# The end of a transformer block rebuilt: last products row block by row block, right halves prepared early, eight output buffers

## The chip, the cores and the metric

The kernel runs on one core of one Trainium2 chip. It is one launch that computes one whole layer. The metric is device time in microseconds (us), the median of several executions of the same program.

A core has five engines that run their own instruction queues and wait for each other through semaphores: TensorE (PE in the profile) multiplies matrices into PSUM banks, VectorE (DVE) and ScalarE (ACT) do elementwise work, GpSimd (POOL) does slower elementwise work, and SyncE (SP) issues DMA transfers between the core's SBUF and the device's memory. Each engine runs its queue strictly in order: an instruction that waits holds up everything behind it on that engine.

## What is computed

One layer on an input x of 1024 positions by 1024 channels: a normalised, modulated input goes through a state-space mixer and a chunked attention, then a convolutional feed-forward network, and a last RMS norm. Only the end matters here:

```python
def rmsnorm(x, w):
    y = x * lax.rsqrt(jnp.mean(x * x, axis=-1, keepdims=True) + EPS)
    return y * w
...
        x = x + g_f * conv_ffn(h, w_up[l], ffn_conv_w[l], w_down[l])
    return rmsnorm(x, final_norm_w)
```

The last step of `conv_ffn` is a product of a (1024 x 2816) matrix with `w_down` (2816 x 1024). Its result is multiplied by the gate `g_f`, x is added, and every row of 1024 numbers is divided by its root mean square and weighted with `final_norm_w`. A row's scale is known only when both of its halves of 512 columns are complete.

## The kernel before

**The product.** The down projection is done as a Strassen-like scheme: the (1024 x 2816) by (2816 x 1024) product is cut into 2 x 2 blocks, and seven products of half size, in the order P1, Q5, Q6, Q7, Q4, P3, P2, stand in place of eight. Each product works on 11 steps of 128 along the contracted dimension (`KH`), loaded in six pieces m = 0 to 5 of two steps, the last of one (`NM`, `kn`). Each result is four row blocks of 128 x 512 numbers in four PSUM banks (`banks("d")` and `banks("e")` alternate). For precision every float32 operand is split into a high part (ACT, line 85) and a low part (DVE, line 86), and `mm3` (lines 76 to 78) issues three matmuls per step and row block: high by high, high by low, low by high. `split_pair` makes the split parts of one piece in tiles of a ring of five (`ring`), so a split can start only when TensorE has done with the piece that used the ring tile before.

**The rows.** There are eight row blocks of 128 positions and two column halves. Four lists of four tiles of 128 x 512 gather the results: `q5` is the right half of row blocks 4 to 7 and is complete after Q7; `u3` is the right half of row blocks 0 to 3 and is complete after Q4; `u2` is the left half of row blocks 4 to 7 and is complete after P3; `p1` is the left half of row blocks 0 to 3 and is complete after P2. `gate` (lines 1408 to 1413) multiplies a tile by the gate `gf` and adds x, which a DMA brings into one of two buffers `xts`.

**The last product.** `product("P2", W, tail=True)` issues steps 0 to 7 and returns the last three (pieces 4 and 5) in `last`. At the end a loop over the four row blocks of rows 0 to 3 issues for each row block its nine matmuls, a multiplication by the gate into `e` (line 1493), the addition to `p1` (line 1494) and `final`.

**`final`** (lines 1415 to 1424) squares both halves on ACT into the output tile with a running sum (line 1419; each is an ACTIVATE and a small ACTIVATION_READ_ACCUMULATOR), combines the two sums on DVE (line 930) and raises to the power -0.5 on POOL (line 931, in `rstd2`), scales and weights each half in one DVE instruction with the scale and the weights `fnr` (line 1422), and sends each half out with a DMA on SP (line 1424). Its output tile is one of three, `fins`.

**What sets the order.** The program states dependencies; a planner that simulates a timeline orders each engine's queue, so instructions of the end may be placed ahead of or between others than the text has them, and the nine matmuls of the four row blocks may be mixed. Two things pin the order by hand: `tc.issue_after`, and the wrapper `InOrder`, which while its `on` is true makes each instruction of an engine follow the one before it in the text (its issues are then recorded under line 58).

Of the kernel before, what the change touches and what calls it, by code (L numbers as in the profile page):

```python
# [12 lines left out]
AF = mybir.ActivationFunctionType  # L13
ALU = mybir.AluOpType
PSUM = bass.MemoryType.PSUM

P = 128
# [47 lines left out]
def tile_block(ctx: ExitStack, tc: tile.TileContext, x, crep, pk, w_ada, w_first, w_ft, w_z,  # L65
               w_out, w_up, w_down, bias, fnw, out, dbg=None):
    nc = tc.nc
    V, A, T = (InOrder(tc, e) for e in (nc.vector, nc.scalar, nc.tensor))
    G = nc.gpsimd
# [36 lines left out]
    def stat(n=1):  # L106
        if stc[0] + n > 64:
            stc[0] = 0
        a = st1[:, stc[0]:stc[0] + n]
        stc[0] += n  # L110
        return a
# [15 lines left out]
    def raw_tile(n=1024):  # L127
        rawc[0] += 1
        return raws[:, rawc[0] % 2, 0:n]
# [199 lines left out]
    for hh in range(2):  # L329
# [4 lines left out]
        for kt in range(KT):  # L334
            if hh == 0:
# [4 lines left out]
                t = raw_tile(768)  # L340
# [50 lines left out]
    ya = yp.tile([P, NT, 512], F32, tag="y", name="ya")  # L391
# [147 lines left out]
    xs = xsp.tile([P, NT, 512], F32, name="xs")  # L539
# [60 lines left out]
    halves = [slice(0, 512), slice(512, 1024)]  # L600
# [202 lines left out]
    def ssd_y(c, xdt, xdd, cb, ms_):  # L803
        cs = slice(c * P, (c + 1) * P)
        prev, cur = state[c % 2], state[(c + 1) % 2]
        ydp = ssd_tile("ydp")
        for h in range(8):
            pe(T.matmul, ydp[:, h * 64:h * 64 + 64], ms_[h // 4][:, h % 4, :],
               xdt[:, h * 64:h * 64 + 64], start=True, stop=True)
        y = sp.tile([P, 512], F32, tag="yy", bufs=2, name="yy")  # L810
        G.tensor_tensor(h8(y), h8(xs[:, c, :]),
                        pkt[:, DSK:DSK + 8].unsqueeze(2).to_broadcast([P, 8, 64]), ALU.mult)
        t = sp.tile([P, 512], F32, tag="yt", bufs=2, name="yt")
        if c > 0:
            yop = ssd_tile("yop")
            for g in range(2):
                pe(T.matmul, yop[:, g * 256:g * 256 + 256], ct_[g][:, cs], prev[:, g * 256:g * 256 + 256],
                   start=True, stop=True)
        if c < NT - 1:
            stp = ssd_tile("stp")  # L820
            for g in range(2):
                pe(T.matmul, stp[:, g * 256:g * 256 + 256], cb[:, 2 + g, :],
                   xdd[:, g * 256:g * 256 + 256], start=True, stop=True)
            if c > 0:
                G.tensor_tensor(h8(cur), h8(prev), hb("cd", c), ALU.mult)
                V.tensor_tensor(cur, stp, cur, ALU.add)
            else:
                A.activation(cur, stp, AF.Copy)
        V.tensor_tensor(y, ydp, y, ALU.add)
        if c > 0:  # L830
            V.tensor_tensor(h8(t), h8(yop), hb("ea", c), ALU.mult)
            V.tensor_tensor(y, y, t, ALU.add)
        return y, t
# [21 lines left out]
    def kn(m):  # L855
        return min(2, KH - 2 * m)

    gd = {}
    for m in range(NM):
        for n, names in (("x", ("b11",)), ("y", ("t1", "t3")), ("z", ("t2", "t4", "b21", "b22"))):  # L860
            t = gd[n, m] = dram.tile([kn(m), P, len(names), 512], F32, name=f"g{n}{m}")
# [66 lines left out]
    def rstd2(m):  # L928
        ms, r = stat(), stat()
        V.scalar_tensor_tensor(ms, m[0], EPS, m[1], op0=ALU.add, op1=ALU.add)  # L930
        G.tensor_tensor(r, ms, mhalf[:, 0:1], ALU.pow)  # L931
        return r
# [4 lines left out]
    for c in range(NT):  # L937
        y, t = ssd_y(c, *pre)
# [85 lines left out]
    def wsplit(src, n=2):  # L1024
# [5 lines left out]

    PRODS = dict(P1=(0, "b11", "X"), P2=(1, "b21", "X"), Q4=(2, "t4", "Y"), Q5=(4, "t1", "Z"),
                 Q6=(5, "t2", "Y"), Q7=(6, "t3", "Y"), P3=(7, "b22", "Z"))

    class Unit:
# [23 lines left out]
        def product(self, p, post=True):  # L1058
            _, n, t = PRODS[p]
            start = t not in self.ps  # L1060
            if start:
                self.ps[t] = (psz if t == "Z" else ps3).tile([P, 512], F32, tag=t, bufs=2, name="u" + t)
            ps, w, h = self.ps[t], self.w[p], hb_[n]
            for kt in range(4):
                c = slice(kt * P, (kt + 1) * P)
                mm3(ps, w[:, 0, c], w[:, 1, c], h[0][:, kt, :], h[1][:, kt, :],
                    start and kt == 0, kt == 3, not start)
            if post:
                self.post(p)

        def post(self, p):
# [12 lines left out]
            elif p == "Q7":  # L1084
                V.tensor_tensor(self.v[:, 512:S], ps, self.v[:, 0:512], ALU.subtract)
                V.tensor_tensor(self.v[:, 512:S], self.v[:, 512:S], self.ps["Z"], ALU.subtract)
            elif p == "Q4":
# [78 lines left out]
    row = lambda u, o: (lambda: u.sums((o,)))  # L1166
# [51 lines left out]
    lo = [u.prep("Q7", "Q4", True) for u in units]  # L1218
# [31 lines left out]
    def buf(name, n=D):  # L1250
        if name not in bufs:
            home = next(h for h in HOME if name in HOME[h][1])
            pool, names = HOME[home]
            t = pool.tile([P, 1024 * (1 if home == "s0" else 4 if pool is htp else 2)], F32,
                          tag="a" if pool is hp else home, bufs=2 if pool is hp else 1,
                          name="dn" + home)
            o = 0
            for g in names:
                w = 512 if g.endswith("_5") else 1024
                bufs[g] = t[:, o:o + w]  # L1260
                o += w
        return bufs[name][:, 0:n]
# [80 lines left out]

    gf, fnr = (t[:, 0:2, :].rearrange("p a b -> p (a b)") for t in (ya, xs))
    q5 = [ya[:, 2 + st, :] for st in R4]
    fins = [t[:, j:j + 2, :].rearrange("p a b -> p (a b)") for t, j in ((xs, 2), (xs, 4), (ya, 6))]
    xts = [xs[:, 6 + j, :] for j in range(2)]
    BANK = dict(zip(("e2", "e3", "d0", "d1", "d2", "d3", "e0", "e1"), range(8)))
    for t in BANK:
# [2 lines left out]
    def banks(t):  # L1352
        return [ps4.tile([P, 512], F32, tag=f"{t}{st}", name="dn") for st in R4]
# [31 lines left out]
    def step(ps, ab, k, sts):  # L1385
        a, b = (t[:, :, k % 2, :] for t in ab)
        for st in sts:
            c = slice(st * P, (st + 1) * P)
            mm3(ps[st], b[:, 0, c], b[:, 1, c], a[:, 0, :], a[:, 1, :], k == 0, k == KH - 1)
# [14 lines left out]
    def xt_():  # L1404
        xc[0] += 1
        return xts[xc[0] % 2]

    def gate(t, st, dh):
        V.tensor_tensor(t, t, gf[:, halves[dh]], ALU.mult)
        x = xt_()  # L1410
        with tc.issue_after(last_load[0]):
            nc.sync.dma_start(x, x1d[st * P:(st + 1) * P, halves[dh]])
        V.tensor_tensor(t, t, x, ALU.add)

    def final(st, lo, hi):
        t = fins[st % 3]
        m = [stat(), stat()]
        for dh, src in enumerate((lo, hi)):
            A.activation(t[:, halves[dh]], src, AF.Square, scale=1.0 / 32.0, accum_out=m[dh])
        r = rstd2(m)  # L1420
        for dh, src in enumerate((lo, hi)):
            V.scalar_tensor_tensor(t[:, halves[dh]], src, r, fnr[:, halves[dh]], op0=ALU.mult,
                                   op1=ALU.mult)
            nc.sync.dma_start(out[st * P:(st + 1) * P, halves[dh]], t[:, halves[dh]])

    def rows(ts):
        return [t[:, 512 * j:512 * j + 512] for t in ts for j in range(2)]
# [37 lines left out]
    u3 = rows([buf("u30"), buf("u31")])  # L1465
    for st in R4:
        V.tensor_tensor(u3[st], X[st], u2[st], sub)
    for st in R4:
        V.tensor_tensor(u2[st], u2[st], q5[st], ALU.add)
        V.tensor_tensor(q5[st], u3[st], q5[st], sub)  # L1470
    for st in R4:
        gate(q5[st], 4 + st, 1)
    nc.sync.dma_start(fnr, fnw)
    X = banks("d")
    product("Q4", X)
    for st in R4:
        V.tensor_tensor(u3[st], u3[st], X[st], ALU.add)
    for st in R4:
        gate(u3[st], st, 1)
    Z = banks("e")  # L1480
    product("P3", Z)
    W = banks("d")
    last = product("P2", W, tail=True)
    for st in R4:
        V.tensor_tensor(u2[st], u2[st], Z[st], ALU.add)
    for st in R4:
        gate(u2[st], 4 + st, 0)
        final(4 + st, u2[st], q5[st])
    for st in R4:
        for ab, k in last:  # L1490
            step(W, ab, k, (st,))
        e = xt_()
        V.tensor_tensor(e, W[st], gf[:, halves[0]], ALU.mult)
        V.tensor_tensor(p1[st], p1[st], e, ALU.add)
        final(st, p1[st], u3[st])
    es_s.close()
    es_ht.close()
    es_l.close()
# [51 lines left out]
```

## Time and profile before

| what | before |
|---|---|
| median of 3 runs | 1222.43 us (1222.42 to 1225.11) |
| profiled execution, span from first to last instruction | 1221.2 us |
| mean granted TensorE clock | 0.993 |
| POOL busy in the span | 174.3 us |
| multiplications of two 128 x 512 tiles on POOL (lines 708, 811) | 1.12 and 1.36 us mean |
| `fnr` load (line 1473): issued, landed | 1045.4 us, 7.7 us later |
| right-half squares of row blocks 4, 5, 6 (line 1419) | 1130.65, 1135.86, 1136.49 us |

The profiled execution's own time is known by its span alone, 1221.2 us; the median of the runs is 1.2 us above that, for what lies around the first and the last instruction.

A row of the timeline gives start, duration, engine, line, operation, output tile <- input tiles, shapes, and in brackets the idle time before it with what ended that. Rows of one kind that follow each other are merged (x2, x4), and their duration then reaches from the first start to the last end. Output tiles called `dn` on PE are PSUM banks; `cg` holds `p1`, `cv` holds `u2`, `st` the row sums and scales; `xs` and `ya` are two large tiles that hold `gf`, `fnr`, `q5`, `fins` and the buffers `xts`; `dnH` holds `u3` among other things. A window row gives, for one stretch, the busy time of each engine with its count of instructions, then granted clock, share of the DMA engines and GB/s.

### The profile page before, as it was taken

The numbers are of one execution on the slowest core, as the hardware profiler recorded it, in microseconds if no ns is written. First come the engines' busy times: TensorE is split into PE (matmuls) and PEld (weight loads), VectorE is DVE, ScalarE is ACT, GpSimd is POOL, SyncE is SP. The second block draws the span as 40 slices with busy tenths as digits, with TensorE's granted clock in tenths as the row PEclk, the third lists the DMA queues.
The fourth block names the chain that finished last, engine by engine and source line by source line (L and its number), as shares of the span: only waits on it lengthen the run. The fifth ranks groups of instructions, "written<-read, shape, count | busy, mean of one in ns | idle before, by whom it ended". The sixth has DMA issues, their size and how long they took to land.

```text
span 1221.2 us, 15631 instructions
## 1 busy us (share of the span) xinstructions
PE 1167.3 (96%) x5802; PEld 974.5 (80%) x5802; DVE 928.8 (76%) x1402; ACT 592.0 (48%) x993; POOL 174.3 (14%) x166
## 2 busy tenths in 40 slices
PE   5998899989999989999999999999999999999995
PEld 3877787878889978888788888888888888888884
DVE  7846454686697678657999988898889769666976
ACT  4636454664243766676544543344343445433443
POOL 1205463672000125200000000000000000000001
PEclk9999999999999999999999999999999999999998
DMA  9722211311476200141223223322233278633533
GB/s 331 259 56 63 66 54 46 111 58 51 164 246 229 88 18 35 61 147 52 70 104 118 93 107 113 129 79 86 95 129 112 108 250 305 242 126 116 171 114 137
DMA packets 56395, 150.86 MB, mean 124 GB/s; under 512 B 5632, under 2 KB 5760, under 8 KB 54912
## 3 DMA queue, kind: packets, MB, share of 16 engines
q1 hardware_dynamic: 49264, 125.49, 30.4%
q10 hardware_dynamic: 7056, 24.38, 5.0%
q8 instruction: 45, 0.74, 0.2%
q14 instruction: 30, 0.25, 0.1%
HBM read 116.56 MB, written 29.10 MB: 119 GB/s over the span
## 4 chain that ended last, share of the span: by engine, by line
PE 82%; DVE 9%; ACT 3%; issue 2%; DMA 2%; POOL 1%; SPq 0%; DVEq 0%; POOLq 0%; ACTq 0%
PE dn L76 6%; PE dn L77 6%; PE dn L78 6%; PE wops L699 5%; PE uY L76 4%; PE uY L78 4%; PE uY L77 4%; PE uX L78 3%; PE uX L76 3%; PE uZ L77 3%; PE uZ L76 3%; PE uX L77 3%; PE uZ L78 3%; PE s L76 3%; PE s L77 3%; PE s L78 3%
## 5 line engine op out<-in xcount | busy, mean ns | idle before, releaser
L77 PE MATMUL dn<-w 128*128 128x512 f32 x308 | 112.6, 391 | 0.0
L76 PE MATMUL dn<-w 128*128 128x512 f32 x308 | 112.6, 391 | 0.0
L931 POOL TENSOR_TENSOR st<-st,mhalf 128x1 f32<-128x1 f32 x16 | 10.9, 683 | 696.1 <-DVE st L930 684.6
L419 POOL TENSOR_SCALAR p<-p,st 128x640 f32<-128x640 f32 (+4 forms) x64 | 99.0, 1560 | 43.7 <-DVE st L418 36.4
L78 PE MATMUL dn<-w 128*128 128x512 f32 x308 | 103.7, 390 | 0.0
L76 PE MATMUL uY<-tH,w 128*128 128x512 f32 x248 | 97.2, 392 | 0.0
L77 PE MATMUL uY<-tL,w 128*128 128x512 f32 x248 | 97.0, 391 | 0.0
L78 PE MATMUL uY<-tH,w 128*128 128x512 f32 x248 | 96.9, 391 | 0.0
L85 ACT ACTIVATE w<-ya 128x1024 fp32r<-128x1024 f32 (+1 forms) x41 | 39.2, 956 | 87.4 <-PE uY L78 84.2
L699 PE MATMUL wops<-hH,yhl 128*128 128x512 f32 x224 | 74.1, 399 | 2.9 <-DVE yhl L86 1.5
L76 PEld LDWEIGHTS dn<-w 128*128 128x128 f32 x308 | 57.8, 188 | 12.9
L78 PEld LDWEIGHTS dn<-w 128*128 128x128 f32 x308 | 57.8, 188 | 12.8
L77 PEld LDWEIGHTS dn<-w 128*128 128x128 f32 x308 | 57.8, 188 | 12.7
L85 ACT ACTIVATE w<-xs 128x1024 fp32r<-128x1024 f32 (+1 forms) x41 | 39.1, 953 | 37.3 <-PE uY L78 33.3
L78 PEld LDWEIGHTS uY<-tH,w 128*128 128x128 f32 x248 | 46.5, 188 | 10.5
L76 PEld LDWEIGHTS uY<-tH,w 128*128 128x128 f32 x248 | 46.6, 188 | 10.3
L77 PEld LDWEIGHTS uY<-tL,w 128*128 128x128 f32 x248 | 46.6, 188 | 10.2
L413 DVE CUSTOM_DVE_ANT_0 p<-s,bias 128x640 f32<-128x640 f32 (+4 forms) x64 | 40.4, 651 | 17.5 <-PE tp L445 5.2
L76 PE MATMUL s<-hH,wh 128*128 128x512 f32 x128 | 50.1, 392 | 2.2 <-ACT xst L518 2.0
L86 DVE TENSOR_TENSOR pt<-tp,pt 128x512 fp32r<-128x512 f32 (+2 forms) x72 | 41.5, 595 | 13.1 <-ACT pt L85 12.8
L699 PEld LDWEIGHTS wops<-hH,yhl 128*128 128x128 f32 x224 | 41.8, 188 | 12.2 <-DVE yhl L86 1.9
L1101 DVE SCALAR_TENSOR_TENSOR a<-cv,pkt,a 128x1023 f32<-128x1023 f32 (+1 forms) x40 | 51.0, 1278 | 0.1
(453 smaller groups left out, 3388.9 us busy)
## 6 DMA issues: line engine op xcount, KB each, us to landing
wos<-in_w_ada_dram SPq DMA_DIRECT2D x25, 512.0 KB, 4.5
gz<-a ACTq DMA_DIRECT2D x10, 1024.0 KB, 5.0
ya<-in_w_up_dram SPq DMA_DIRECT2D x11, 768.0 KB, 4.1
xs<-in_w_up_dram SPq DMA_DIRECT2D x11, 768.0 KB, 4.2
adat<-in_w_ada_dram SPq DMA_DIRECT2D x16, 512.0 KB, 5.9
raws<-in_w_ft_dram SPq DMA_DIRECT2D x14, 512.0 KB, 4.0
gy<-a ACTq DMA_DIRECT2D x10, 512.0 KB, 2.6
qk<-in_x_dram SPq DMA_DIRECT2D x8, 512.0 KB, 6.6
```

The lines of the kernel that those rows point to most:

```text
L76: T.matmul(ps, lh, rh, start=start, stop=False, skip_group_check=more)
L77: T.matmul(ps, lh, rl, start=False, stop=False, skip_group_check=more)
L78: T.matmul(ps, ll, rh, start=False, stop=stop, skip_group_check=more)
L85: i = A.activation(hi, src, AF.Copy) if ehi is A else ehi.tensor_copy(hi, src)
L86: return i, elo.tensor_tensor(lo, src, f32(hi), ALU.subtract)
L413: V.tensor_tensor_reduce(out=dst, in0=src, in1=bsl, scale=-1.0, scalar=3e38, op0=ALU.add, op1=ALU.min, accum_out=nm)
L419: G.tensor_scalar(pv_, pv_, rr, None, op0=ALU.mult)
L699: i = op(*a, **k)
L931: G.tensor_tensor(r, ms, mhalf[:, 0:1], ALU.pow)
L1101: V.scalar_tensor_tensor(a[:, j:S], c[:, 0:S - j], w[2 - j], a[:, j:S], op0=ALU.mult, op1=ALU.add)
```

## The change

Four edits, all in the code after the feed-forward's first half.

- The 36 last matmuls of P2 are issued in the order of the text: row block 0 with all nine, then 1, 2, 3 (`T.on`).
- The right halves of all row blocks are squared as soon as they are gated, and multiplied in place by the right half of `fnr` on POOL (`right_half`). The statement of the `fnr` load stands ahead of that.
- `final` squares only the left half. Its right half is scaled by ACT (an activation Copy with a scale per row), its left half still by DVE. The right half is sent first.
- The output tile of each row block is its own, in memory that earlier products no longer need (`buf("a11_0")` and so on), in place of three in turn; squares go into six `junk` tiles, and `e` is one of those in place of a buffer of `xts`.

In the built program the `fnr` load has the same place in SP's queue as before, DVE's order differs only from the first line 1422 on, ACT's gets the early squares and the copies, POOL's gets eight multiplications ahead of its last eight powers, and PE's differs in the last 36 matmuls alone.

```diff
-    fins = [t[:, j:j + 2, :].rearrange("p a b -> p (a b)") for t, j in ((xs, 2), (xs, 4), (ya, 6))]
+    junk = [t[:, j, :] for t, j in ((xs, 2), (xs, 3), (xs, 4), (xs, 5), (ya, 6), (ya, 7))]
...
-    def final(st, lo, hi):
-        t = fins[st % 3]
-        m = [stat(), stat()]
-        for dh, src in enumerate((lo, hi)):
-            A.activation(t[:, halves[dh]], src, AF.Square, scale=1.0 / 32.0, accum_out=m[dh])
-        r = rstd2(m)
-        for dh, src in enumerate((lo, hi)):
-            V.scalar_tensor_tensor(t[:, halves[dh]], src, r, fnr[:, halves[dh]], op0=ALU.mult,
-                                   op1=ALU.mult)
-            nc.sync.dma_start(out[st * P:(st + 1) * P, halves[dh]], t[:, halves[dh]])
+    jc, sq = [0], {}
+
+    def junk_():
+        jc[0] += 1
+        return junk[jc[0] % 6]
+
+    def square(row, dh, src):
+        sq[row, dh] = stat()
+        A.activation(junk_(), src, AF.Square, scale=1.0 / 32.0, accum_out=sq[row, dh])
+
+    def right_half(row, src):
+        square(row, 1, src)
+        G.tensor_tensor(src, src, fnr[:, halves[1]], ALU.mult)
+
+    def final(row, lo, hi):
+        t = buf(("a11_0", "a11_1", "a11_2", "a11_3", "a22_0", "a22_1", "a22_2", "a22_3")[row])
+        square(row, 0, lo)
+        r = rstd2((sq[row, 0], sq[row, 1]))
+        A.activation(t[:, halves[1]], hi, AF.Copy, scale=r)
+        V.scalar_tensor_tensor(t[:, halves[0]], lo, r, fnr[:, halves[0]], op0=ALU.mult, op1=ALU.mult)
+        for dh in (1, 0):
+            nc.sync.dma_start(out[row * P:(row + 1) * P, halves[dh]], t[:, halves[dh]])
...
+    nc.sync.dma_start(fnr, fnw)
     for st in R4:
         gate(q5[st], 4 + st, 1)
-    nc.sync.dma_start(fnr, fnw)
+        right_half(4 + st, q5[st])
...
     for st in R4:
         gate(u3[st], st, 1)
+        right_half(st, u3[st])
...
+    T.on, T.last = True, None
     for st in R4:
         for ab, k in last:
             step(W, ab, k, (st,))
-        e = xt_()
+        e = junk_()
         V.tensor_tensor(e, W[st], gf[:, halves[0]], ALU.mult)
         V.tensor_tensor(p1[st], p1[st], e, ALU.add)
         final(st, p1[st], u3[st])
+    T.on = False
```

## The prediction

> **What bounds the kernel now.** I read the page's busy times first, then the busy time by stretches over the down projection, then the chain that ended last, then the timelines of the last 25 us engine by engine, and last the waits.
>
> ```profile
> PE 1167.3 (96%) x5802; PEld 974.5 (80%) x5802; DVE 928.8 (76%) x1402; ACT 592.0 (48%) x993; POOL 174.3 (14%) x166
> ```
> ```profile
> 1117.00:1147.00 30.00, 30.00 (x133) 24.58 (x131) 27.40 (x35) 13.05 (x19) 0.00 (x0) 1.00 0.42 140
> 1147.00:1177.00 30.00, 30.00 (x132) 24.57 (x131) 23.23 (x29) 11.17 (x12) 0.00 (x0) 1.00 0.54 176
> 1199.00:1207.40 8.40, 8.40 (x37) 6.57 (x35) 2.91 (x5) 2.08 (x5) 0.00 (x0) 1.00 0.24 92
> 1207.40:1221.20 13.80, 0.01 (x1) 0.00 (x0) 9.56 (x19) 3.45 (x10) 2.70 (x4) 0.62 0.40 152
> ```
>
> TensorE is busy without a gap until 1207.4, and then does nothing for the last 13.8 us. The change adds no matmul and takes none away, so all it can win lies in those 13.8 us, and all it can lose ahead of them is a gap in TensorE's row. In 1199 to 1207.4 DVE works 2.9 us of 8.4: the end's elementwise work has not begun. The chain says why:
>
> ```profile
> 1205.82 0.47 PE dn L78 x2
> ...
> 1206.31 1.29 DVE xs L1493 x2
> ...
> 1211.34 2.65 DVE xs L1422 x4
> ...
> 1216.87 0.75 DVE xs L1422
> ```
>
> TensorE mixes the matmuls of the four row blocks, so the first result is ready at 1206.3, hardly before the last. Then DVE works off four row blocks, and one square waits for an output buffer (longest wait in the third number):
>
> ```profile
> ACT xs L1419 <- DMA out_dram<-xs: 4.1, 2, 2.7
> ```
>
> **Row block order.** The 36 last matmuls run from the first to the last of these rows:
>
> ```profile
> 1199.02 0.39 PE L76 MATMUL dn<-w 128*128 128x512 f32 x1
> ...
> 1207.03 0.39 PE L78 MATMUL dn<-w 128*128 128x512 f32 x1
> ```
>
> Their pitch is (1207.03 - 1199.02) / 35 = 0.229 us, nine are 2.06 us. In order, the row blocks end at 1201.24 (1199.02 + 8 x 0.229 + 0.39), 1203.30, 1205.36 and 1207.42. The same matmuls, so TensorE's end stays at 1207.42.
>
> **What a row block costs behind TensorE.** Durations and pitches come from these rows:
>
> ```profile
> 1208.86 0.61 ACT L1419 ACTIVATE xs<-cg 128x512 f32<-128x512 f32 x1
> 1209.31 0.68 DVE L1493 TENSOR_TENSOR xs<-dn,ya 128x512 f32<-128x512 f32 x1
> 1209.38 0.19 ACT L1419 ACTIVATION_READ_ACCUMULATOR xs<-cg 128x1 f32 x1
> 1209.91 0.15 DVE L930 SCALAR_TENSOR_TENSOR st<-st 128x1 f32<-128x1 f32 x1
> 1209.98 0.69 DVE L1494 TENSOR_TENSOR cg<-cg,xs 128x512 f32<-128x512 f32 x1
> 1210.14 0.93 POOL L931 TENSOR_TENSOR st<-st,mhalf 128x1 f32<-128x1 f32 x1 [11.38 <-DVE st L930]
> 1216.28 0.55 POOL L931 TENSOR_TENSOR st<-st,mhalf 128x1 f32<-128x1 f32 x1 [1.60 <-DVE st L930]
> 1216.87 0.75 DVE L1422 SCALAR_TENSOR_TENSOR xs<-cg,st,xs 128x512 f32<-128x512 f32 x1 [0.66 <-POOL st L931]
> 1217.54 0.75 DVE L1422 SCALAR_TENSOR_TENSOR xs<-dnH,st,xs 128x512 f32<-128x512 f32 x1
> ```
>
> On DVE the gate multiplication holds the queue 0.60 (1209.31 to 1209.91), the combination 0.07, a scaling 0.66; an addition takes 0.69 to its end. A square with its sum read is 0.73, an ACT pass without the sum 0.62. The power takes 0.55 alone, and 0.93 when an addition starts just before it, as at 1209.98: then it ends 0.41 after the addition's end (1211.07 against 1210.67). From one engine to the next I take 0.03, to POOL 0.08 (1210.06 to 1210.14).
>
> In the built order DVE does: gate 0, add 0, gate 1, combine 0, add 1, scale 0, gate 2, combine 1, add 2, scale 1, and so on; ACT does square 0, copy 0, square 1, copy 1. Row block 0: gate 1201.28, add 1201.88 to 1202.57, square and sum to 1203.33. Gate 1 starts when row block 1 is done, 1203.34; combine 0 at 1203.94, add 1 from 1204.01 to 1204.70, the power until 1205.11, scale 0 at 1205.15. From here one scale follows the other by 0.66 + 0.60 + 0.07 + 0.69 + 0.41 + 0.03 = 2.46, more than TensorE's 2.06, so DVE with the power is the bound: scale 1 at 1207.61, scale 2 at 1210.07. (The square behind a copy on ACT, 1205.15 + 0.53 + 0.73 = 1206.41, comes just in time for its combination; it costs 0.02.) The last row block: copy 2 from 1210.07, square 3 with its sum until 1211.34, combination until 1211.52, power alone until 1212.15, scale 3 from 1212.18 to 1212.93, the right half's copy from 1212.18 to 1212.80.
>
> **The outputs.** Sixteen transfers as before, two per row block, on SP; each landed about 2.0 us after its issue, so none waits for another. Two issues lie 0.52 apart (0.89 for a pair, less an issue of 0.33 to 0.37) when both are ready:
>
> ```profile
> 1141.00 0.89 SPq L1412 DMA_DIRECT2D xs<-x1d  x2
> ...
> 1218.31 0.33 SPq L1424 DMA_DIRECT2D out_dram<-xs  x1
> ```
>
> The right half is issued at 1212.83, the left at 1213.35. Before, the last issue was at 1218.31. What follows it, 2.9 us to 1221.2, stays. **The sum: 1213.35 - 1218.31 = -4.96**, a span of 1216.2; the median of the runs stands 1.2 above the profiled span, so 1217.5.
>
> **Separate output buffers** take away the wait of 2.7 on the old chain; with the order changed, the sum above holds no wait for a buffer, so nothing is added for it. The three-buffer wait of 1.4 at 1202 was on ACT alone and cost nothing. `e` in a junk tile frees the buffers of `xts`: nothing.
>
> **Scaling the right half on ACT** takes eight 0.75 off DVE and puts eight of 0.62 on ACT. For the rows 4 to 7 this lies in 1188 to 1199, under TensorE; for the others it is in the sum, where it shortens the cycle by 0.66. Left on DVE the cycle would be 3.1.
>
> **Early squares.** Three of the eight stood early already; the other five add 5 x 0.8 = 4 us to ACT, which works 13 and 11 of 30 us in the two windows above. A split behind one of them is at most 0.8 late, less than the smallest margin below (1.39). Nothing.
>
> **Eight multiplications on POOL** are the step that can cost. POOL is idle there, but DVE slows beside it, as the state-space stage shows (a row of DVE, one of POOL):
>
> ```profile
> 444.53 1.53 DVE L716 TENSOR_TENSOR rm<-tle,adl 128x512 fp32r<-128x512 f32 x1
> ```
> ```profile
> 444.02 1.49 POOL L811 TENSOR_TENSOR yy<-xs,pkt 128x512 f32<-128x512 f32 x1
> ```
>
> A DVE instruction on two 128 x 512 tiles, 0.68 at 1209.31, took 1.53 beside a POOL multiplication of 1.49: 0.85 lost. In the window 1117 to 1147 DVE's idle time is 30 - 27.4 = 2.6, all of it in one wait just before 1145.38, and four multiplications fall ahead of that: 4 x 0.85 = 3.4 us. The lower bound of a multiplication's price is 0 (DVE waits for something else anyway), the upper 1.49 (DVE stands still for all of it); I take the row, 0.85. What covers it:
>
> ```profile
> 1145.38 1.23 DVE L86 TENSOR_TENSOR w<-dnL,w 128x1024 fp32r<-128x1024 f32 x1 [2.60 <-ACT w L85]
> ...
> 1157.00 1.22 DVE L86 TENSOR_TENSOR w<-dnL,w 128x1024 fp32r<-128x1024 f32 x1
> ```
> ```profile
> 1159.61 0.63 PE L78 MATMUL dn<-w 128*128 128x512 f32 x2
> ```
>
> DVE then waits 2.60 for ACT, and the low part it makes from 1157.00 to 1158.22 is wanted only by the L78 at 1159.61: 1.39 more. Up to 3.99 us TensorE sees nothing; 3.4 is under that. The second four fall in 1161 to 1172, where DVE is idle 30 - 23.2 = 6.8 us of its window. So 0, with 1.39 + 2.60 as the margin. Were that cover gone, it would be 6.8 us.
>
> [...]
>
> **Rivals.** First, row block 0 waits for the last split. In text order its seventh matmul already needs the half piece 5, whose ring tile comes free only when TensorE is done with piece 3:
>
> ```profile
> 1199.28 0.63 ACT L85 ACTIVATE w<-dna 128x512 fp32r<-128x512 f32 x1 [1.95 <-PE dn L78]
> ```
> ```profile
> 1188.71 0.68 DVE L1413 TENSOR_TENSOR cv<-cv,xs 128x512 f32<-128x512 f32 x1
> ...
> 1200.13 0.69 DVE L86 TENSOR_TENSOR w<-dna,w 128x512 fp32r<-128x512 f32 x1
> ```
>
> The high part is there at 1199.91, wanted at 1200.39; the low part at 1199.94 + 0.69 = 1200.63, wanted at 1200.85. The margin is 0.2 us, and two copies that wait for POOL stand ahead of it on ACT, one scaling on DVE. They belong to row blocks whose last half is complete at 1189.4 (1188.71 + 0.68), ten us sooner. If they are late all the same, all four row blocks shift; 2 us late gives 1219.5.
>
> Second, POOL holds DVE for whole instructions: 4 x 1.49 = 5.96 less 3.99 is a gap of 2.0 us in TensorE near 1159, and 1219.5.
>
> Third, the row blocks don't overlap on DVE, each runs alone: 0.60 + 0.69 + 0.73 + 0.15 + 0.63 + 0.75 + waits 0.2 = 3.75 a row block. The last scale starts at 1205.15 + 3 x 3.75 = 1216.4 against 1217.54: -1.1, 1221.3. Against it stands the built order, with gate 1 ahead of combine 0.
>
> Fourth, slower: the POOL multiplications starve the splits. It decides from 3.99 us of DVE delay in the first four; to eat the 4.96 and 0.3% (3.67) more, they must delay DVE by 12.6, 3.2 each. At 3.5 each it is 14.0 - 3.99 = 10.0 us of gap and 1227.5. The longest two-input row on POOL is 1.5 for this size, so it has little for it.
>
> Better than the sum: if row block 3 queued behind nothing, gate at 1207.45, add to 1208.74, square to 1209.50, combine to 1209.68, power to 1210.31, scale at 1210.34, issues at 1210.99 and 1211.51: -6.8, 1215.6.
>
> **How the numbers follow.** The forecast has 0.72, the first rival 0.08, the second 0.08, the third 0.08, the fourth 0.04. The forecast's own bounds are 1215.6 (just above) and 1218.7 (0.3 more per cycle and step). The first two rivals reach 1219.5; with a little for their sizes the range is 1215.5 to 1220.0. A difference of 0.3% (3.7 us, 1218.76) is about what a measurement tells from none. The forecast's case counts as faster, with 0.01 from a small first rival: 0.73; the rest of the first three as same: 0.22; slower 0.05.
>
> **What would show it.** PE rows without a gap up to about 1207.4, and the four row blocks' gate multiplications at about 1201.3, 1203.3, 1205.8 and 1208.3; scales of the left halves about 2.5 apart; the last output issue near 1213.4; DVE rows of 1.5 or longer beside POOL near 1131 to 1142 and 1161 to 1172. The prediction is wrong if TensorE shows a gap near 1159 or at 1200, if the scales are over 3 apart, or if something behind the last issue grows.

## The result and the profile after

The changed kernel takes 1220.67 us (median of 22 runs, 1218.94 to 1224.7); the kernel before, run beside it, 1224.34 us (22 runs, 1221.96 to 1229.63). The ratio is 0.997 with an interval of 0.9963 to 0.9977: faster by 3.7 us, where 1217.5 us and a gain of 4.96 us were predicted, and 0.7 us above the top of the range. The kernel before is 1.9 us higher here than the median of three runs that the prediction started from (1222.43), and the gain is 1.3 us smaller.

Whole times scatter by more than these steps are worth: in the ten different kernels of this study the first matmul of the down projection starts anywhere from 993.8 to 999.9 us, with the work ahead of it unchanged. So the profiled executions are compared from that matmul to the end of the span, 225.57 us before, and the stage is cut into three: 924 matmuls back to back, TensorE's gaps between them (every matmul's start to the next's, what is over 0.234 us), and what follows the last matmul.

These are the first matmul of the down projection, before and then after:

```profile
995.60 0.39 PE L76 MATMUL dn<-w 128*128 128x512 f32 x1
```
```profile
995.70 0.39 PE L76 MATMUL dn<-w 128*128 128x512 f32 x1
```

The changed kernel's busy times on the page, and the stretches that answer to those shown of before (length, then busy time and count of PE, PEld, DVE, ACT and POOL, then granted clock):

```profile
PE 1167.9 (96%) x5802; PEld 974.4 (80%) x5802; DVE 927.8 (76%) x1394; ACT 597.0 (49%) x1001; POOL 199.9 (16%) x174
```
```profile
1117.00:1147.00 30.00, 30.00 (x133) 24.59 (x132) 27.40 (x34) 13.73 (x20) 15.45 (x4) 1.00 0.43 140
1147.00:1177.00 30.00, 29.76 (x130) 23.72 (x129) 25.65 (x28) 13.47 (x20) 8.96 (x5) 1.00 0.53 176
1199.00:1208.34 9.34, 9.34 (x41) 7.32 (x39) 5.61 (x10) 2.69 (x6) 1.60 (x2) 1.00 0.17 63
1208.34:1217.70 9.36, 0.00 (x0) 0.00 (x0) 3.78 (x7) 3.39 (x7) 1.79 (x3) 0.63 0.53 199
```

Two things differ from before. Behind TensorE's end 9.39 us are left of 13.76, and DVE does 5.6 us of work under the last matmuls where it did 2.9: the overlap came. But TensorE is no longer full from 1147 to 1177, and POOL is busy for 15.45 us with four instructions in the window before.

| from the first `dn` matmul | before | after |
|---|---|---|
| to TensorE's end | 211.81 | 212.64 |
| of it gaps of TensorE | 0.04 | 0.84 |
| behind TensorE's end | 13.76 | 9.39 |
| in all | 225.57 | 222.03 (-3.54) |

**The gaps.** The first two rows are POOL's first multiplication alone and then with the three that follow it; after them stand DVE's last instruction ahead of its wait and the two behind it.

```profile
1131.55 12.47 POOL L1427 TENSOR_TENSOR ya<-ya,xs 128x512 f32<-128x512 f32 x1 [557.67 <-ACT xs L1423]
1131.55 17.23 POOL L1427 TENSOR_TENSOR ya<-ya,xs 128x512 f32<-128x512 f32 x4 [557.67 <-ACT xs L1423]
```
```profile
1141.65 1.22 DVE L86 TENSOR_TENSOR w<-dnH,w 128x1024 fp32r<-128x1024 f32 x1
1145.48 2.14 DVE L86 TENSOR_TENSOR w<-dnL,w 128x1024 fp32r<-128x1024 f32 x1 [2.60 <-ACT w L85]
1147.54 2.32 DVE L1359 TENSOR_TENSOR dnL<-dnL,dnL 128x1024 f32<-128x1024 f32 x1
...
1153.31 1.21 DVE L86 TENSOR_TENSOR w<-dnH,w 128x1024 fp32r<-128x1024 f32 x1
...
1159.13 1.21 DVE L86 TENSOR_TENSOR w<-dnL,w 128x1024 fp32r<-128x1024 f32 x1
```

From 1131 to 1142.87 DVE works without a break, and nothing in that row is longer than before. POOL's first multiplication is open all that time, 12.47 us for an operation that POOL does in 1.29 a little later, and ends at 1144.02, 1.15 us after DVE's row does. The other three then run until 1148.78, past the end of DVE's wait, and two DVE instructions of 1.22 take 2.14 and 2.32: 2.02 us lost. The low part that began at 1151.18 before begins at 1153.31, 2.13 later; 0.10 of that is the later start of the whole stage, so 2.03 are lost. TensorE's rows show what that costs:

```profile
1153.27 1.08 PE L77 MATMUL dn<-w 128*128 128x512 f32 x4
1154.58 1.19 PE L78 MATMUL dn<-w 128*128 128x512 f32 x4 [0.23 <-DVE w L86]
...
1159.28 1.10 PE L77 MATMUL dn<-w 128*128 128x512 f32 x4
1160.39 1.20 PE L78 MATMUL dn<-w 128*128 128x512 f32 x4
```

Four matmuls at the usual 0.23 would have brought L78 at 1154.19; it starts at 1154.58, and the one at 1160.39 is 0.2 late. In the kernel before the same two rows are:

```profile
1151.18 1.22 DVE L86 TENSOR_TENSOR w<-dnH,w 128x1024 fp32r<-128x1024 f32 x1
```
```profile
1154.09 1.07 PE L78 MATMUL dn<-w 128*128 128x512 f32 x4
```

There the low part was done at 1152.40 (1151.18 + 1.22) for an L78 at 1154.09, a slack of 1.69.

**The end.** DVE's rows, then ACT's of the second cycle, then the last two output issues:

```profile
1202.18 0.69 DVE L1508 TENSOR_TENSOR xs<-dn,ya 128x512 f32<-128x512 f32 x1 [0.67 <-PE dn L58]
1202.90 0.69 DVE L1509 TENSOR_TENSOR cg<-cg,xs 128x512 f32<-128x512 f32 x1
1204.26 0.69 DVE L1508 TENSOR_TENSOR xs<-dn,ya 128x512 f32<-128x512 f32 x1 [0.67 <-PE dn L58]
...
1206.12 0.75 DVE L1434 SCALAR_TENSOR_TENSOR dnb11h<-cg,st,xs 128x512 f32<-128x512 f32 x1 [0.44 <-POOL st L931]
1206.79 0.69 DVE L1508 TENSOR_TENSOR ya<-dn,ya 128x512 f32<-128x512 f32 x1
1207.49 0.16 DVE L930 SCALAR_TENSOR_TENSOR st<-st 128x1 f32<-128x1 f32 x1
1207.57 0.68 DVE L1509 TENSOR_TENSOR cg<-cg,ya 128x512 f32<-128x512 f32 x1
1208.69 0.75 DVE L1434 SCALAR_TENSOR_TENSOR dnb11h<-cg,st,xs 128x512 f32<-128x512 f32 x1 [0.44 <-POOL st L931]
...
1211.26 0.75 DVE L1434 SCALAR_TENSOR_TENSOR dnb11l<-cg,st,xs 128x512 f32<-128x512 f32 x1 [0.44 <-POOL st L931]
...
1213.44 0.75 DVE L1434 SCALAR_TENSOR_TENSOR dnb11l<-cg,st,xs 128x512 f32<-128x512 f32 x1 [0.66 <-POOL st L931]
```
```profile
1206.12 0.72 ACT L1433 ACTIVATE dnb11h<-dnH,st 128x512 f32<-128x512 f32 x1 [1.77 <-POOL st L931]
1206.75 0.62 ACT L1423 ACTIVATE ya<-cg 128x512 f32<-128x512 f32 x1
1207.27 0.18 ACT L1423 ACTIVATION_READ_ACCUMULATOR ya<-cg 128x1 f32 x1
```
```profile
1214.19 0.81 SPq L1436 DMA_DIRECT2D out_dram<-dnb11l  x2
```

The scales of the left halves follow each other by 2.57, 2.57 and 2.18 us. The gate multiplication holds DVE for 0.70 (1206.79 to 1207.49) where 0.60 was taken: the square's sum arrives at 1207.45, because ACT's scaling before it takes 0.72 and not 0.62. ACT starts this square at 1206.75, behind the scaling, though its input was there at 1205.68 (1204.99 + 0.69). The last issue begins at 1214.61, and 3.1 us later the span ends.

### The profile page after: what moved, and what is told of

Its sections match the earlier page's. It is cut to its first block, busy times and chain, and to the rows that moved or that the text cites. A ratio compares the mean times of both kernels' runs of the same rounds, so it can differ in the third digit from the quotient of the medians.

```text
span 1217.7 us, 15636 instructions
## 1 busy us (share of the span) xinstructions
PE 1167.9 (96%) x5802; PEld 974.4 (80%) x5802; DVE 927.8 (76%) x1394; ACT 597.0 (49%) x1001; POOL 199.9 (16%) x174
## 4 chain that ended last, share of the span: by engine, by line
PE 80%; DVE 10%; ACT 4%; DMA 2%; issue 2%; POOL 1%; SPq 0%; POOLq 0%; DVEq 0%; ACTq 0%
PE wops L699 5%; PE dn L78 5%; PE dn L76 5%; PE dn L77 5%; PE uY L76 5%; PE uY L78 5%; PE uY L77 4%; PE uX L78 3%; PE uX L76 3%; PE uZ L77 3%; PE uX L77 3%; PE uZ L76 3%; PE uZ L78 3%; PE s L76 3%; PE s L77 2%; PE s L78 2%
## 5 line engine op out<-in xcount | busy, mean ns | idle before, releaser
L1427 POOL TENSOR_TENSOR ya<-ya,xs 128x512 f32<-128x512 f32 x4 | 17.2, 4334 | 557.7 <-ACT xs L1423 557.7
L77 PE MATMUL dn<-w 128*128 128x512 f32 x296 | 108.1, 392 | 0.0
L76 PE MATMUL dn<-w 128*128 128x512 f32 x296 | 108.1, 391 | 0.0
L78 PE MATMUL dn<-w 128*128 128x512 f32 x296 | 100.2, 391 | 0.2 <-DVE w L86 0.2
L78 PE MATMUL uY<-tH,w 128*128 128x512 f32 x248 | 96.9, 391 | 0.0
L78 PEld LDWEIGHTS dn<-w 128*128 128x128 f32 x296 | 55.4, 188 | 13.3 <-DVE w L86 1.1
L76 PEld LDWEIGHTS dn<-w 128*128 128x128 f32 x296 | 55.5, 188 | 12.3
L77 PEld LDWEIGHTS dn<-w 128*128 128x128 f32 x296 | 55.5, 188 | 12.2
L78 PEld LDWEIGHTS uY<-tH,w 128*128 128x128 f32 x248 | 46.5, 188 | 10.4
L86 DVE TENSOR_TENSOR pt<-tp,pt 128x512 fp32r<-128x512 f32 (+2 forms) x72 | 41.5, 595 | 13.2 <-ACT pt L85 12.8
```

Source lines behind the costliest of these rows:

```text
L76: T.matmul(ps, lh, rh, start=start, stop=False, skip_group_check=more)
L77: T.matmul(ps, lh, rl, start=False, stop=False, skip_group_check=more)
L78: T.matmul(ps, ll, rh, start=False, stop=stop, skip_group_check=more)
L86: return i, elo.tensor_tensor(lo, src, f32(hi), ALU.subtract)
L1427: G.tensor_tensor(src, src, fnr[:, halves[1]], ALU.mult)
```

## The experiments

All times of stages are worked out as in the table above; "in all" is from the first `dn` matmul to the end of the span, and the number in brackets its difference from before.

**The right halves back on DVE.** Nothing is multiplied on POOL; the early squares, the buffers and the order stay.

```diff
     def right_half(row, src):
         square(row, 1, src)
-        G.tensor_tensor(src, src, fnr[:, halves[1]], ALU.mult)
...
-        A.activation(t[:, halves[1]], hi, AF.Copy, scale=r)
+        V.scalar_tensor_tensor(t[:, halves[1]], hi, r, fnr[:, halves[1]], op0=ALU.mult, op1=ALU.mult)
```

> The changed kernel with the eight POOL multiplications taken out: right_half only squares, and final scales and weights both halves on DVE as before. Theory (the POOL multiplications hold DVE at 1145 to 1149 and so open the two gaps in TensorE's row at 1154 and 1160): no gap, TensorE ends near 1207.4 and not 1208.3; each row block costs DVE one 0.66 more, so the end behind TensorE grows from 9.3 to about 10.7 us, span near 1218.1. Rival (the early squares on ACT delay the splits): the gaps stay, TensorE ends near 1208.3, span near 1219.

Measured: ratio 0.9985 (0.9968 to 1.0001), gaps 0.05, end 10.24, in all 222.10 (-3.47). Without POOL's eight multiplications, and with the early squares still in place, the gaps are gone: the multiplications make them. The end is 0.85 longer than the changed kernel's. The two nearly cancel: moving the right halves to POOL and ACT won 0.85 at the end and lost 0.80 in the middle. DVE's cycle with both scalings was put at 3.1 us; here the left halves' scales follow by 3.25, 2.74 and 2.15, since the gate of row block 3 (1206.09) is placed ahead of scale 1. DVE's rows of this kernel:

```profile
1204.10 0.75 DVE L1433 SCALAR_TENSOR_TENSOR dnb11h<-cg,st,xs 128x512 f32<-128x512 f32 x1
...
1206.09 0.68 DVE L1507 TENSOR_TENSOR xs<-dn,ya 128x512 f32<-128x512 f32 x1
...
1207.35 0.74 DVE L1433 SCALAR_TENSOR_TENSOR dnb11h<-cg,st,xs 128x512 f32<-128x512 f32 x1
...
1210.09 0.75 DVE L1433 SCALAR_TENSOR_TENSOR dnb11l<-cg,st,xs 128x512 f32<-128x512 f32 x1
...
1212.24 0.75 DVE L1433 SCALAR_TENSOR_TENSOR dnb11l<-cg,st,xs 128x512 f32<-128x512 f32 x1
```

**The order alone**, put into the kernel before:

```diff
+    T.on, T.last = True, None
     for st in R4:
         for ab, k in last:
...
+    T.on = False
```

> The kernel before with one edit: the last 36 matmuls in the order of the text, row block by row block. Theory (the order is what wins, the rest about cancels): TensorE ends at 1207.4, scales follow each other at about 3.2 us, last output issue about 3 us earlier than the 1218.3 of before, span near 1218.1. Rival (the three output buffers or the late squares eat it): an ACT wait for an output transfer stands on the chain and the span is above 1219.5.

Measured: 0.9967 (0.9955 to 0.9979), gaps 0.16, end 10.24, in all 222.20 (-3.37). This one of the four edits does nearly all that the whole change does. The left halves' scales follow by 3.26, 2.74 and 2.15 us, where about 3.2 was expected, and ACT's wait of 2.7 us for an output buffer does not occur.

**The change without the order:**

```diff
-    T.on, T.last = True, None
     for st in R4:
```

> The changed kernel without the order of the last matmuls. Theory (order wins): gaps in TensorE at 1154 and 1160 as in the changed kernel, first gate multiplication at about 1207.2, all four row blocks' work and eight output issues after that, span 1218.7 or more, so at least 1 us slower than the changed kernel. Rival (early right halves and separate buffers are what wins): span near 1217.7, as the changed kernel.

Measured: 1.0002 (0.9988 to 1.0016), gaps 0.84 at the same places as in the changed kernel, end 11.80, in all 224.43 (-1.14). Without the order the other parts are worth 1.96 at the end, less the gaps. The outputs bunch here: the last five are issued on SP within 3.1 us.

**The multiplications on DVE**, where the changed kernel has them on POOL:

```diff
-        G.tensor_tensor(src, src, fnr[:, halves[1]], ALU.mult)
+        V.tensor_tensor(src, src, fnr[:, halves[1]], ALU.mult)
```

> The changed kernel with the eight multiplications of right_half on DVE in place of POOL. Theory (it is the lock with POOL, late and in a bunch, that hurts, not the work): 4 x 0.6 = 2.4 us on DVE ahead of its wait of 2.6 at 1145, so the wait swallows it; no gap in TensorE, TensorE ends at 1207.4, the end as in the changed kernel, span near 1216.8. Rival (DVE is full there and any work on it opens a gap): gaps of 0.5 us or more near 1154 to 1160, span 1217.5 or more.

Measured: 0.9961 (0.9944 to 0.9978), gaps 0.05, end 9.38, in all 221.23 (-4.34). DVE itself can carry them; its wait of 2.60 shrinks to 0.19 and TensorE sees nothing (the window row, then DVE's row behind the wait):

```profile
1117.00:1147.00 30.00, 30.00 (x133) 24.59 (x132) 29.81 (x38) 13.84 (x21) 0.00 (x0) 1.00 0.41 130
```
```profile
1144.76 1.22 DVE L86 TENSOR_TENSOR w<-dnL,w 128x1024 fp32r<-128x1024 f32 x1 [0.19 <-ACT w L85]
```

So 2.4 us of DVE's own work ahead of the wait costs nothing, and 2.0 us lost to POOL behind it costs 0.8. By whole times the intervals of this kernel and the changed one overlap; it is the stage that is 0.80 us shorter.

**Every POOL multiplication twice**, the added one into a tile that is written again later:

```diff
         square(row, 1, src)
+        G.tensor_tensor(buf(f"a11_{row % 4}")[:, halves[1]], src, fnr[:, halves[1]], ALU.mult)
         G.tensor_tensor(src, src, fnr[:, halves[1]], ALU.mult)
```

> The changed kernel with each POOL multiplication done twice (the first time into a scratch tile, so the result stays). Theory (POOL first starves behind DVE's unbroken row until DVE's wait near 1143, and what is left over in a bunch then holds DVE): the first multiplication again ends near 1144, seven more follow until about 1153, DVE is late by about 2.1 + 4 x 1.0 = 6.2 us where it was 2.1, and TensorE's gaps near 1154 to 1160 grow from 0.8 to between 4 and 5.5 us; the end behind TensorE stays 9.3. Rival (the gaps come from the early squares on ACT): gaps of 0.8 as before.

Measured in one execution: 1227.22 us against a median of 1224.34, gaps 4.30, end 9.38, in all 225.56 (0.0). The rows are POOL's first two and DVE's three around the wait:

```profile
1135.18 13.09 POOL L1427 TENSOR_TENSOR dnb11h<-ya,xs 128x512 f32<-128x512 f32 x1 [557.09 <-DVE ya L1413]
1148.35 1.29 POOL L1428 TENSOR_TENSOR ya<-ya,xs 128x512 f32<-128x512 f32 x1
```
```profile
1145.90 1.22 DVE L86 TENSOR_TENSOR w<-dnH,w 128x1024 fp32r<-128x1024 f32 x1
1149.73 2.25 DVE L86 TENSOR_TENSOR w<-dnL,w 128x1024 fp32r<-128x1024 f32 x1 [2.60 <-ACT w L85]
1151.90 2.32 DVE L1359 TENSOR_TENSOR dnL<-dnL,dnL 128x1024 f32<-128x1024 f32 x1
```

Again the first one ends 1.15 us after DVE's row (1148.27 against 1147.12), and what is left hits DVE behind its wait. Twice the work on POOL costs 5 times the gap here. Of the 4.30 us only 3.1 lie at the two places of before (here 1158.2 to 1167, as the stage starts 4.2 us later), less than the 4 to 5.5 expected there; the other 1.2 lie between 1177 and 1188, beside the second four multiplications, where the changed kernel has no gap.

**DVE's row broken by instructions that read PSUM.** Four instructions more on DVE than the changed kernel has, each with one of its two inputs in PSUM:

```diff
-        V.tensor_tensor(t, t, x, ALU.add)
+        return V.tensor_tensor(t, t, x, ALU.add)
...
-        gate(q5[st], 4 + st, 1)
+        done = gate(q5[st], 4 + st, 1)
         right_half(4 + st, q5[st])
+        with tc.issue_after(done.ins):
+            V.tensor_tensor(junk_(), X[st], gf[:, halves[0]], ALU.mult)
```

> The changed kernel with four more instructions on DVE, one right behind each gate addition of the rows 4 to 7 (about 1131, 1137, 1138, 1142): each multiplies a PSUM tile by an SBUF tile into a junk tile nobody reads, 0.6 us of queue each, so that DVE's row of instructions with two SBUF inputs is broken three times while POOL's first multiplication is under way. Theory (that row starves POOL, POOL gets in only where DVE does something else): the first multiplication, 12.5 us long in the changed kernel and over 1.1 us behind DVE's falling idle, ends near 1138, 1 to 1.5 us behind the second of the new instructions, though DVE is busier than before; the next ones take their turns at the other two and hit DVE inside the row. DVE then has 2.4 of own work and some 2 of losses against the wait of 2.6, so TensorE's gaps come out near those of the changed kernel, 0.4 to 1.5 us. Rival (POOL is slow for a reason of its own, or waits for DVE's queue to run dry): the first multiplication again ends about 1.1 us behind the moment at which DVE falls idle, now near 1145, so near 1146.4, and the others follow there, where the wait is only 0.2 us long: gaps of 2.5 us or more. The end behind TensorE 9.4 in both.

Measured in one execution of each: 1221.23 us against 1224.94, gaps 1.66, end 9.39, in all 222.92 (-2.65). POOL's first multiplication, then DVE's rows around the time at which it ends:

```profile
1132.44 6.13 POOL L1427 TENSOR_TENSOR ya<-ya,xs 128x512 f32<-128x512 f32 x1 [557.66 <-ACT xs L1423]
```
```profile
1136.74 0.68 DVE L1413 TENSOR_TENSOR ya<-ya,xs 128x512 f32<-128x512 f32 x1
1137.34 0.68 DVE L1488 TENSOR_TENSOR ya<-dn,ya 128x512 f32<-128x512 f32 x1
1137.94 1.18 DVE L1413 TENSOR_TENSOR ya<-ya,xs 128x512 f32<-128x512 f32 x1
1139.04 0.68 DVE L1488 TENSOR_TENSOR xs<-dn,ya 128x512 f32<-128x512 f32 x1
1139.64 1.71 DVE L86 TENSOR_TENSOR w<-dns,w 128x1024 fp32r<-128x1024 f32 x1
```

The first multiplication ends at 1138.57, 1.23 us after the start of the PSUM read at 1137.34, in the middle of DVE's row: 6.13 us in place of 12.47, on a DVE with more to do. This is what the theory said and the rival excluded. The second one ends at 1140.27, again 1.23 us after the start of a PSUM read (1139.04). The gaps, 1.66, are a little above the 1.5 of the theory and below the 2.5 of the rival.

The third multiplication does not fit the theory. It gets its turn between two DVE instructions with both inputs in SBUF that follow each other without a break, and the second of these loses 1.1 us:

```profile
1142.09 1.56 POOL L1427 TENSOR_TENSOR ya<-ya,xs 128x512 f32<-128x512 f32 x1 [1.82 <-ACT ya L1423]
```
```profile
1141.28 1.21 DVE L1359 TENSOR_TENSOR dnH<-dnH,dnt1h 128x1024 f32<-128x1024 f32 x1
1142.42 1.78 DVE L86 TENSOR_TENSOR w<-dnb21l,w 128x512 fp32r<-128x512 f32 x1
```

The changed kernel has both cases too: a multiplication open from 1170.12 is through in 1.44 us between two L86, the second of which takes 1.78 us where others of its size take 0.69; one open from 1163.51 takes 3.19 us and ends at 1166.70, 1.15 us after the end of the L86 of 1164.34 (1165.55). So at both PSUM reads of this row POOL's multiplication ended 1.23 us after the read's start, but an unbroken row did not always keep it out (1.56 and 1.44 us), and what decides is not shown.

**The buffers alone**, in the kernel before:

```diff
-    def final(st, lo, hi):
-        t = fins[st % 3]
+    def final(row, lo, hi):
+        t = buf(("a11_0", "a11_1", "a11_2", "a11_3", "a22_0", "a22_1", "a22_2", "a22_3")[row])
```

> The kernel before with one edit: each row block has its own output tile. Theory (the wait for a buffer was hardly on the path, DVE's queue is): the 2.7 us wait of ACT for an output transfer is gone, but the last issue comes only about 0.8 us earlier, end behind TensorE near 13.0 where it was 13.8, ratio 0.999 to 1.000. Rival (the buffer wait was on the path in full): the end shortens by 2.7 us to 11.1, ratio near 0.998.

Measured: 0.9986 (0.9973 to 1.0), gaps 0.05, end 12.30, in all 224.12 (-1.45). It lies between what the two sides expected, so neither is borne out. The last scaling on DVE, 8.6 us behind TensorE's end at 1207.62 (before, 1217.54 - 1207.41 = 10.1):

```profile
1216.24 0.75 DVE L1422 SCALAR_TENSOR_TENSOR dnb11l<-dnH,st,xs 128x512 f32<-128x512 f32 x1
```

**A longer tail.** The multiplications on DVE, and the last five steps of P2 (60 matmuls) row block by row block in place of three, for which the split parts of the last pieces get tiles of their own; four outputs move to other tiles.

```diff
-    def wsplit(src, n=2):
-        w = ring()[:, :, 0:n, :]
+    def wsplit(src, n=2, w=None):
+        w = ring()[:, :, 0:n, :] if w is None else w
...
+    def own(p, m):
+        if p != "P2" or m < 4:
+            return None, None
+        w = hc1.tile([P, 2, 2, 512], F32R, tag="b11h" if m == 4 else "b11l", bufs=1, name="w")
+        return (None, w) if m == 4 else (w[:, :, 0:1, :], w[:, :, 1:2, :])
...
-        ab = [wsplit(t, kn(m)) for t in operands(p, m)]
+        ab = [wsplit(t, kn(m), w) for t, w in zip(operands(p, m), own(p, m))]
...
-                if tail and m >= NM - 2:
+                if tail and m >= NM - 3:
```

> The kernel with the multiplications on DVE and one edit more: the last five steps of P2 in place of three are issued row block by row block (60 matmuls), with own tiles for the split parts of the last pieces so that the ring of five does not hold them up; the outputs of row blocks 0 to 3 go to other free memory. Theory (DVE's 2.57 us a row block against TensorE's 2.06 is what queues up at the end): 15 matmuls take 3.43 us a row block, DVE keeps up, and behind TensorE's last matmul stands one row block alone, 0.73 + 0.69 + 0.73 + 0.15 + 0.65 + 0.75 and waits of 0.3 until its last scale, then an issue 0.4 later and 3.0 to the end: end behind TensorE near 7.5 us, span near 1214.9, ratio 0.9935 to 0.995. Rival (the row blocks are bound by something else, or the order opens a gap in TensorE): end 8.8 us or more, or a gap over 0.5 us near 1193.

Measured: 0.996 (0.9943 to 0.9976), gaps 0.05, end 7.94, in all 219.91 (-5.66). The end is 0.4 longer than the theory's 7.5 and the ratio above its 0.995, but well clear of the rival's 8.8. It was then run once more on one chip with the changed kernel:

> The changed kernel once more, beside the next one on one chip. POOL's first multiplication again over 12 us long and ending about 1.1 us behind DVE's falling idle, two TensorE gaps of 0.8 us together, 9.4 us behind the last matmul: 222.0 us from the down projection's first matmul to the end, 3.5 less than before.

> The version with the multiplications on DVE and the last five steps of P2 row block by row block, beside the changed kernel on one chip: no TensorE gap, 7.9 us behind the last matmul, 219.9 us of stage, 2.1 less than the changed kernel and 5.7 less than before. If the whole times carry that, its ratio is some 0.0017 below that of the changed kernel, 0.9955 against 0.997; if the earlier stages scatter by more than that, the two intervals overlap and only the stage tells them apart.

Measured: the changed kernel 1219.67 us (12 runs), 0.9972 (0.996 to 0.9985), its first multiplication 12.48 us, gaps 0.85, end 9.39, in all 222.04; the longer tail 1218.56 us (6 runs), 0.9964 (0.995 to 0.9977), gaps 0.06, end 7.93, in all 219.91. The stages repeat to 0.01 us and stand 2.13 apart; the intervals of the whole times overlap, so by whole times this version beats the kernel before, but not yet the changed one. DVE's last row block in it:

```profile
1207.48 0.69 DVE L1514 TENSOR_TENSOR xs<-dn,ya 128x512 f32<-128x512 f32 x1 [0.50 <-PE dn L58]
1208.09 0.74 DVE L1440 SCALAR_TENSOR_TENSOR dnL<-cg,st,xs 128x512 f32<-128x512 f32 x1
1208.75 0.68 DVE L1515 TENSOR_TENSOR cg<-cg,xs 128x512 f32<-128x512 f32 x1
...
1211.11 0.75 DVE L1440 SCALAR_TENSOR_TENSOR dnL<-cg,st,xs 128x512 f32<-128x512 f32 x1 [0.66 <-POOL st L931]
```

With 3.4 us of matmuls per row block DVE is no longer the bound. One scale of the row block before still stands between gate and addition, 0.66 us; the rest is one row block's own chain and the output.

## Why the prediction was right and wrong

**Right: where the gain lies, and how it comes about.** All of it lies behind TensorE, the row blocks overlap on DVE, and the order is what makes them do so (3.37 of 3.54 by itself; the whole change without it only 1.14). DVE with the power is the bound at the end: 2.57 us a row block, where TensorE's results come 2.08 apart (1202.18 and 1204.26). The first rival, row block 0 waiting for the last split, did not come: the last 36 matmuls have no gap in the changed kernel, and one of 0.1 us in the kernel with the order alone. The third, no overlap, fell with the rows of the end; the fourth, slower, with the ratio. The early squares cost nothing, as said (gaps 0.05 with them).

**Wrong: "So 0, with 1.39 + 2.60 as the margin", the step on the eight POOL multiplications.** It cost 0.80 us. The size of the loss was put too high, 4 x 0.85 = 3.4 against 0.92 + 1.10 = 2.02, and it would have been covered at either size where it was expected, ahead of DVE's wait. What failed is the place. The prediction had POOL slow DVE down in the row from 1131 to 1142. In fact POOL's first multiplication, open from 1131.55, ended only at 1144.02, 1.15 us after DVE's row; the other three followed until 1148.78, and the loss fell behind the wait. The 2.60 could not cover it; only the slack of the low parts could, 1.69 for the first. 2.03 - 1.69 is 0.34, and with 0.05 from the low part's end to the matmul the first L78 is 0.39 late; the late L78 at 1160.39 is the next 0.2, and most of the rest is the slower pitch (0.34 in place of 0.23) behind each of the two matmuls that restart. In the run with PSUM reads in this row the first multiplication took 6.13 us in place of 12.47; the runs with the right halves or the multiplications on DVE, both with gaps of 0.05, show that the gaps go with the multiplications on POOL. Why POOL's first multiplication, open from 1131.55, saw twelve more DVE instructions start before it ended, and the one of 1170.12 only one, stays open. The second rival had the right direction, POOL holding up DVE, at 2.0 us and at one place, but not the mechanism.

The prediction took the 0.85 of the L716 row as a price well under the 1.49 of the POOL instruction beside it. That DVE instruction came up at 444.53, when the POOL instruction of 444.02 had 0.98 left, and lost 0.85; the two of the changed kernel came up 1.06 and 1.24 before POOL's ends at 1146.54 and 1148.78 and lost 0.92 and 1.10. So in all three DVE lost nearly all of what POOL had left, and the size of the loss followed from when DVE came up.

**Mis-sized: the cycle, 2.46 against 2.57, 2.57 and 2.18 for the last (2.11 predicted).** The term is ACT's copy, taken as a pass without sum at 0.62; with a scale per row it takes 0.72, so the next square's sum comes 0.10 later, and a gate holds DVE for 0.70. The prediction said it "comes just in time". Together this is 0.29 over three cycles. Also the addition starts 0.72 to 0.73 after its own gate, whose result it reads, and not 0.60 (1202.18 and 1202.90, 1204.26 and 1204.99); this makes the first scale 0.05 late.

**Mis-sized: what follows the last issue, 2.86 against 3.11**, 0.25 us. The two last issues lie 0.42 apart here and 0.66 in the kernel before, so the end comes 3.52 to 3.54 us behind the last issue but one in both. The same holds for the kernels with the order alone and with the right halves on DVE (0.66 to 0.67 apart, 2.87 to the end) and for the one with the multiplications on DVE (0.42, 3.10): sending the last half sooner after the one before it did not bring the end sooner. With the buffers alone the end comes 2.91 us behind the last issue, and without the order, where the last five stand within 3.1 us, 3.80. Why is not shown. Together with 0.29 and with 0.05 at the first scale this makes the end 9.39 where 8.8 followed from the sum: 0.6. With 0.8 of gaps that is 1.4, the difference between -4.96 and -3.54.

**The base.** The sum was set on a median of three runs; the median of 22, with these three among them, is 1.9 us higher. With -4.96 in full the time would have been 1219.4 from the new base, and with the measured gain of 3.67 it would have been 1218.8 from the old one. Both lie inside the range: the time left it by the smaller gain and the higher base together, and the range had no term for the base. The 1.2 us between span and median, said to lie around the first and last instruction, compared different executions; each execution on record with both numbers stands 1.67 to 2.02 us above its own span. In the sum this cancels.

**Separate buffers** were given nothing with the order, and 1.45 is what they are worth without it: the two gains overlap, 1.45 + 3.37 against 3.47 for order, buffers and early squares together. **Scaling on ACT** was to shorten the cycle by 0.66; over three cycles that is 2.0, and 0.82 came (7.32 us against 8.14), because DVE's order without it hides part of the second scaling. The left half's scale also comes 0.68 sooner behind TensorE's end, and what follows the last scale is 0.65 longer; that leaves the 0.85 of the end.

## What to carry to other kernels

Before work moves to an engine beside which the bound one has been slower (DVE took 1.53 us for 0.68 beside POOL), look at what the bound engine does while the moved work is to run: here an unbroken row on DVE went with 12.47 us for the 1.29 us of POOL's multiplication, the rest of the work fell behind the next wait, and the slack that counted was the 1.69 us behind that wait, not the 2.60 of the wait itself. An engine that looks 91% busy may still be the cheaper place, if its idle time lies where the work is (here 2.4 us on DVE for nothing against 0.8 us of TensorE from POOL). And where TensorE ends far ahead of the program, the order of its last matmuls is the first thing to try: it gave 3.4 us with two lines, and more matmuls per row block gave another 1.4 behind TensorE.

## What was not expected of the hardware

POOL's 128 x 512 multiplication took 1.29 us in DVE's wait, but the first one was open for 12.47, 12.48 and 13.09 us in three executions (the changed kernel twice, and the one with every multiplication twice) while DVE ran instructions with two inputs in SBUF without a break, and each time it ended 1.15 us after DVE fell idle. With PSUM reads of 0.68 us in DVE's row it was open for 6.13 us and ended 1.23 us after the start of one. Elsewhere a multiplication was through without either, in 1.44 and 1.56 us between two DVE instructions with both inputs in SBUF. The two 1.22 us instructions of DVE that came up while POOL's multiplications were open behind its wait took 2.14 and 2.32 us in the changed kernel and 2.25 and 2.32 with every multiplication twice, 0.9 to 1.1 us more. ACT's Copy of 128 x 512 with a scale per row took 0.72 us in the end's cycle where the squares beside it took 0.61 to 0.63.
